# Encoder layer with expert-choice MoE on one core: the last stage summed in PSUM for all four column quarters

## The chip, the cores and the metric

The kernel runs on one core of a Trainium2 chip. The metric is the device time of one execution in microseconds (us), the median of several runs. The engines are TensorE (PE in the profile, with its weight loads as PEld), VectorE (DVE), ScalarE (ACT), GpSimd (POOL) and SyncE (SP), which issues most of the transfers. Matmuls of fp32 operands appear in the profile as two records each, those of fp32r operands as one.

## The reference, cut to what matters

One layer: three token mixers, a residual LayerNorm, then an expert-choice mixture of 16 SwiGLU experts and a second residual LayerNorm. There are 512 tokens of width 1024; each expert takes 64 tokens.

```python
def expert_choice_ffn(x, w_router, w_gate_up, w_down):
    ...
    gate, idx = lax.top_k(jnp.swapaxes(aff, 1, 2), cap)
    xs = x[bidx, idx]
    h = jnp.einsum('becd,edf->becf', xs, w_gate_up)
    hg, hu = jnp.split(h, 2, axis=-1)
    ye = jnp.einsum('becf,efd->becd', jax.nn.silu(hg) * hu, w_down)
    ye = ye * gate[..., None].astype(ye.dtype)
    return jnp.zeros_like(x).at[bidx, idx].add(ye)
...
ffn = expert_choice_ffn(x, w_router[l], w_gate_up[l], w_down[l])
x = layer_norm(DN_ALPHA * x + ffn, ln2_g[l], ln2_b[l])
```

`layer_norm` subtracts the mean over the 1024 columns, divides by the deviation (the square root of variance plus 1e-5), multiplies by a gain row g and adds a bias row b.

## The kernel before, in words

Instructions go to each engine in program order; the order of the program text is the order of every engine's queue. PSUM has eight banks of 128x512 fp32, handed out in turn under four tags: `mm` (3 banks), `S` (2), `T` (2) and `Y` (1). A new tile of a tag waits until the readers of the tile that had its bank are done.

The experts' weights come by a ring of SBUF tiles (`Ring`, L749): each `get` hands out a loaded piece, each `done` lets SP issue the next load. In order: for each expert eight pieces of gate and up weights and, for the expert before, four pieces of down weights; at the end the four down pieces of expert 14 and the four of expert 15. The pieces of expert 15 are laid out by column quarters: piece q holds all the rows of `w_down` for columns 256q to 256q+255.

Per expert e: `gate_up` (L1194) multiplies the gathered tokens (64 columns of `xs`) with gate and up weights, two column halves of 512 side by side into partitions 0-63 and 64-127 of a bank; `act_h` (L1208) makes the activation; `h_transpose` (L1217) turns it by TensorE; `down` (L1226) makes the 64 x 1024 product, split by `hi_lo` (L84) into an fp32r part and an fp32r remainder (a cast on ScalarE, a subtraction on VectorE). For every pair of experts `combine` (L1297) spreads the 128 rows to the tokens with a one-hot matrix (`slots_T`, L1252) and adds them to the accumulators `ACC[0]`, `ACC[1]` (each 128 x 2 x 1024, two blocks of 128 tokens; they start as the scaled residual). `rows_of_norm` (L1310, run in expert 12) puts the second LayerNorm's gain into `g2` and gain and bias as fp32r rows into `gb`.

The last pair (experts 14 and 15) isn't combined that way but in `last_down` (L1340), by column quarters q of 256:

- `product(q)` (L1356): expert 15's down product for quarter q. For each of eight row blocks kk it issues two matmuls of 128 columns, o = 0 and 1, into partitions 64o to 64o+63, in bank `yq` of tag S for even q, T for odd q.
- `split(q)` (L1365): the product into `yh` and `yl`, two casts and two subtractions of 64x128.
- `add(q)` (L1378), for quarters 0 and 1: eight fp32r matmuls of 256 columns into two banks, then VectorE adds them to the accumulators and takes the statistics (`bn_stats`) from SBUF; POOL multiplies by the gain (`times_g`, L1374).
- `add_in_psum(q)` (L1390), for quarters 2 and 3: the eight matmuls add to banks `xq` in which `preload` (L1334, called in expert 15, L1533 and L1538) has put the accumulators by an fp32 product with the identity. Statistics and gain are then read from PSUM by VectorE (L1397, L1400).

Then mean and variance are put together (`bn_aggr`, L1429), the reciprocal deviation y is made by square root, reciprocal and one refining step (L1430 to L1435), and -mean*y, in two fp32r parts beside ones, is written to `ch`, transposed to rows (L1442) and copied (L1444). A matmul with K = 6 of these rows and `gb` (`low_rank`, L1453) gives -mean*y*g + b for every token and column. For five of the eight output pieces (128 tokens x 512 columns, 256 KB) VectorE forms x*y plus that (`by_dve`, L1466) and SP sends them. For the three others (first column half of token blocks 0 to 2) TensorE forms diag(y) times x in fp32 (`diag`, L1458), ScalarE copies the sum (`by_act`, L1471) and sends it. `keep_warm` (L1406) issues matmuls whose results nothing reads, 22 of them after the last add and three before `low_rank`.

Of the kernel before, what the change touches and what calls it, by code (L numbers as in the profile page):

```python
# [9 lines left out]
F32 = mybir.dt.float32  # L10
# [31 lines left out]
def layer_kernel(ctx: ExitStack, tc: tile.TileContext, xt, xn, first0, wu, bgate, rpb, gains, wrt,  # L42
# [201 lines left out]
    gb = cp.tile([6, D], F32R, name="gb")  # L244
# [972 lines left out]
    def h_transpose(e, tp=None):  # L1217
        h = HT[e]
        tp = tp or PB("mm", f"ht{e}", (P, 4, P))
        for c in range(4):  # L1220
            nc.tensor.transpose(tp[:, c], h[:, c * P:(c + 1) * P], ident)  # L1221
        t = R("A6", [P, 4, P], f"hT{e}") if e == NEXP - 1 else R("tmp", [P, 4, P], f"hT{e}", bufs=2)
        HT[e] = t
        nc.vector.tensor_copy(t, tp)  # L1224
# [85 lines left out]
    def rows_of_norm(g2):  # L1310
# [4 lines left out]
        sl, cc = (small([6, 1], n, bufs=1) for n in ("gb_s", "gb_c"))  # L1315
        nc.vector.tensor_tensor(sl, ident[:6, 4:5], ident[:6, 5:6], op=ALU.add)
        nc.vector.tensor_scalar(cc, sl, -2.0, 1.0, op0=ALU.mult, op1=ALU.add)
        sel = small([32, 8, 6], "gb_sel", bufs=1)
        for i in range(2):
            nc.vector.tensor_copy(sel[:, :, i:6:2], ident[:32, 16 + 8 * i:24 + 8 * i, None].to_broadcast([32, 8, 3]))  # L1320
        for h in range(2):
            c = slice(h * 512, h * 512 + 512)
            raw = PB("mm", f"gbr{h}")
            for j in range(4):
                nc.tensor.matmul(raw[:6, j * P:(j + 1) * P], sel[:, 4 * h + j], lnr, start=True, stop=True)
            u = R("t", [P, 512], f"gbu{h}", bufs=2)
            nc.scalar.copy(gb[:, c], raw[:6])
            nc.vector.tensor_scalar(u[:6], gb[:, c].bitcast(F32), cc, None, op0=ALU.mult)
            nc.vector.scalar_tensor_tensor(gb[:, c], raw[:6], sl, u[:6], op0=ALU.mult, op1=ALU.add)
            yield  # L1330

    quarters = [slice(q * 256, q * 256 + 256) for q in range(4)]

    def preload(q, banks):  # L1334
        r = [PB(b, f"xq{q}{mp}", (P, 2, 256)) for mp, b in enumerate(banks)]
        for mp in range(2):
            nc.tensor.matmul(r[mp], ident, ACC[mp][:, :, quarters[q]], start=True, stop=False)
        return r

    def last_down(g2, xq, spare):  # L1340
# [9 lines left out]
        yy = [PB(b, f"yq{b}") for b in "ST"]  # L1350
        cbs = [spare, PB("Y", "cbl")]

        def part(q, o):
            return yy[q % 2][o * 64:o * 64 + 64, (q // 2) * P:(q // 2) * P + P]

        def product(q):  # L1356
            w = [x[:, c] for x in ring.get("dn", e, q) for c in range(4)]
            for kk in range(8):
                hf, c = divmod(kk, 4)
                for o in range(2):  # L1360
                    nc.tensor.matmul(part(q, o), hT[:, c, hf * 64:hf * 64 + 64], w[kk][:, o * P:(o + 1) * P],
                                     start=(kk == 0), stop=(kk == 7))
            ring.done("dn", e, q)

        def split(q):  # L1365
            r = slice(64, 128)
            b = cols[q].start
            cs = [slice(b + o * P, b + (o + 1) * P) for o in range(2)]
            for o in range(2):
                nc.scalar.copy(yh[r, cs[o]], part(q, o))  # L1370
            for o in range(2):
                nc.vector.tensor_tensor(yl[r, cs[o]], part(q, o), yh[r, cs[o]].bitcast(F32), op=ALU.subtract)

        def times_g(mp, q):  # L1374
            x = ACC[mp][:, :, cols[q]]
            nc.gpsimd.tensor_tensor(x, x, g2[:, None, cols[q]].to_broadcast([P, 2, 256]), op=ALU.mult)  # L1376

        def add(q):  # L1378
            for m in range(NT):
                cb = cbs[m // 2][:, m % 2 * 256:m % 2 * 256 + 256]  # L1380
                nc.tensor.matmul(cb, g[:, m], yh[:, cols[q]], start=True, stop=False)
                nc.tensor.matmul(cb, g[:, m], yl[:, cols[q]], start=False, stop=True)
            for mp in range(2):
                x = ACC[mp][:, :, cols[q]]
# [38 lines left out]
        add_in_psum(3)  # L1423
        for mp in range(2):
            times_g_psum(2, mp)
        keep_warm(22)
# [3 lines left out]
        nc.scalar.activation(sg, mv[:, :, 1], AF.Sqrt, bias=eps)  # L1430
        nc.vector.tensor_scalar(hv, mv[:, :, 1], LN_EPS, -0.5, op0=ALU.add, op1=ALU.mult)
# [4 lines left out]
        nc.vector.scalar_tensor_tensor(nm, mv[:, :, 0], -1.0, y, op0=ALU.mult, op1=ALU.mult)  # L1436
        nc.vector.tensor_copy(ch[:, :, 0:5:4], nm[:, :, None].to_broadcast([P, NT, 2]))
        nc.vector.tensor_tensor(ch[:, :, 2], nm, ch[:, :, 0].bitcast(F32), op=ALU.subtract)
        dg = R("tmp", [P, NT, P], "dgr", bufs=2)
        tp = PB("Y", "rowT", (P, NT, P))  # L1440
        for m in range(NT):
            nc.tensor.transpose(tp[:6, m], ch[:, m].bitcast(F32), ident)  # L1442
        rows = R("t", [P, 512], "rows", F32R, bufs=2)
        nc.scalar.copy(rows[:6], flat(tp)[:6])  # L1444
        keep_warm(3)
        for m in range(3):
            nc.scalar.activation(dg[:, m], ident, AF.Copy, scale=y[:, m:m + 1])
        for mp in range(2):
            times_g_psum(3, mp)
        bank = {(0, 1): "T", (1, 1): "S", (2, 1): "mm", (3, 1): "mm", (3, 0): "S", (0, 0): "T", (1, 0): "mm", (2, 0): "Y"}  # L1450
        tl = {}

        def low_rank(m, h, start=True):  # L1453
            if start:
                tl[m, h] = PB(bank[m, h], f"lr{m}{h}")
            nc.tensor.matmul(tl[m, h], rows[:6, m * P:(m + 1) * P], gb[:, h * 512:h * 512 + 512], start=start, stop=True)

        def diag(m):  # L1458
            tl[m, 0] = PB(bank[m, 0], f"lr{m}0")
            nc.tensor.matmul(tl[m, 0], dg[:, m], acc_of(m)[:, 0:512], start=True, stop=False)  # L1460

        def store(m, h):
            c = slice(h * 512, h * 512 + 512)
            (nc.sync if h else nc.scalar).dma_start(out[:, m, c], acc_of(m)[:, c])

        def by_dve(m, h):  # L1466
            x = acc_of(m)[:, h * 512:h * 512 + 512]
            nc.vector.scalar_tensor_tensor(x, x, y[:, m:m + 1], tl[m, h], op0=ALU.mult, op1=ALU.add)
            (nc.sync).dma_start(out[:, m, h * 512:h * 512 + 512], x)

        def by_act(m):  # L1471
            x = acc_of(m)[:, 0:512]
            nc.scalar.copy(x, tl[m, 0])
# [195 lines left out]
```

## Time and profile before

| | us |
|---|---|
| runs: median (lowest to highest of 3) | 982.35 (980.65 to 982.48) |
| the profiled execution, whole | 982.14 |
| its span in the profile | 980.3 |
| weights of expert 15 first used in `last_down` | 948.66 |
| last piece of output issued | 977.52 |

| engine | busy us | share of the span |
|---|---|---|
| TensorE (PE) | 957.3 | 98% |
| VectorE (DVE) | 451.6 | 46% |
| ScalarE (ACT) | 269.2 | 27% |
| GpSimd (POOL) | 75.2 | 8% |

A row of the timeline gives start, length, engine, line, operation, the tile written and the tiles read, shapes, a count of merged instructions, and in brackets the engine's idle time before it and what ended that. Lengths of matmul records hold the way through the array; how many fit into a stretch is read from the starts. The chain of waits goes back from the last instruction to what released each step. The mean granted TensorE clock over the whole span is 0.996 of full speed.

### The profile page before, as it was taken

How to read it: one execution, taken by the hardware profiler on the slowest of the kernel's cores; microseconds unless marked ns; L12 is line 12 of the kernel's file. 1: busy time of each engine (PE TensorE's matmuls, PEld its weight loads, DVE VectorE, ACT ScalarE, POOL GpSimd, SP SyncE). 2: the span in 40 equal slices, each digit the busy share in tenths (PEclk: the TensorE clock that was granted, in tenths of full speed). 3: DMA queues.
4: the chain of work that ended last, by engine and by line, in shares of the span. 5: the costliest groups of instructions: out<-in, count | busy, mean ns of one | idle time of the engine just before them, and what ended most of it. 6: DMA issues, size and time to landing. Idle time of an engine off the chain costs nothing.

```text
span 980.3 us, 13446 instructions
## 1 busy us (share of the span) xinstructions
PE 957.3 (98%) x5448; PEld 624.2 (64%) x5448; DVE 451.6 (46%) x852; ACT 269.2 (27%) x531; POOL 75.2 (8%) x82
## 2 busy tenths in 40 slices
PE   8999899999999999999999999999999999999997
PEld 8899787889888888887885334433343333432355
DVE  6347677665376566246473155331332223231336
ACT  5334345444354454233232010100010001100021
POOL 0002403000032231000021000000000000000001
PEclk9999999999999999999999999999999999999998
DMA  9322111211333322675639999999999999999992
GB/s 356 110 66 66 65 65 43 65 46 64 95 109 103 98 81 87 215 287 204 239 122 421 393 426 427 425 427 426 427 426 425 428 425 427 427 426 426 427 388 86
DMA packets 52318, 251.61 MB, mean 257 GB/s; under 512 B 14080, under 2 KB 14496, under 8 KB 28704
## 3 DMA queue, kind: packets, MB, share of 16 engines
q1 hardware_dynamic: 51680, 249.44, 64.2%
q10 hardware_dynamic: 576, 1.31, 0.3%
q8 instruction: 43, 0.70, 0.3%
q14 instruction: 19, 0.16, 0.0%
HBM read 247.84 MB, written 2.10 MB: 255 GB/s over the span
## 4 chain that ended last, share of the span: by engine, by line
PE 79%; DMA 8%; DVE 6%; ACT 2%; POOL 2%; issue 1%; SPq 0%; DVEq 0%; POOLq 0%; ACTq 0%
PE g L1203 10%; PE u L1203 9%; PE y L1236 8%; DMA gu<-in_wgu 6%; PE gate L253 4%; PE gate L254 4%; PE gate L255 4%; DMA dn<-in_wdn 2%; PE cb L1304 2%; PE ga L1168 1%; PE nqk L253 1%; PE nqk L255 1%; PE nqk L254 1%; PE gy L608 1%; PE pr L253 1%
## 5 line engine op out<-in xcount | busy, mean ns | idle before, releaser
L1203 PE MATMUL g<-gu,xs 128*64 128x512 f32 x512 | 134.7, 604 | 1.2 <-DMA gu<-in_wgu 1.1
L1203 PE MATMUL u<-gu,xs 128*64 128x512 f32 x512 | 131.6, 592 | 0.0
L1236 PE MATMUL y<-dn,hT 128*64 128x512 f32 x480 | 106.4, 593 | 2.4 <-DMA dn<-in_wdn 2.3
L85 ACT CAST y<-y 64x512 fp32r<-64x512 f32 x30 | 17.4, 579 | 241.2 <-PE y L1236 211.3
L86 DVE TENSOR_TENSOR y<-y,y 64x512 fp32r<-64x512 f32 x30 | 20.7, 689 | 136.4 <-ACT y L85 136.4
L1203 PEld LDWEIGHTS u<-gu,xs 128*64 128x64 f32 x512 | 36.8, 137 | 73.1 <-issue 71.7
L1236 PEld LDWEIGHTS y<-dn,hT 128*64 128x64 f32 x480 | 34.0, 137 | 71.5 <-issue 63.5
L86 DVE TENSOR_TENSOR lo_twin<-raw_twin,whi 128x1024 fp32r<-128x1024 f32 x43 | 53.8, 1252 | 51.9 <-ACT whi L85 51.8
L85 ACT CAST whi<-raw_twin 128x1024 fp32r<-128x1024 f32 x64 | 67.2, 1051 | 17.5 <-PE wo L1017 8.7
L1203 PEld LDWEIGHTS g<-gu,xs 128*64 128x64 f32 x512 | 31.3, 136 | 56.0 <-issue 45.3
L1307 DVE TENSOR_TENSOR acc<-acc,cb 128x512 f32<-128x512 f32 x56 | 35.5, 683 | 35.1 <-PE cb L1305 35.1
L86 DVE TENSOR_TENSOR wlo<-raw_twin,whi 128x1024 fp32r<-128x1024 f32 x21 | 27.2, 1295 | 36.8 <-ACT whi L85 36.7
L253 PE MATMUL gate<-xha,whi 128*128 128x512 f32 x96 | 39.0, 406 | 0.0
L1376 POOL TENSOR_TENSOR acc<-acc,ln2g 128x512 f32<-128x512 f32 x4 | 5.1, 1279 | 435.4 <-DVE l2s L1387 435.3
L254 PE MATMUL gate<-xla,whi 128*128 128x512 f32 x96 | 37.5, 391 | 0.0
L253 PE MATMUL gate<-xhb,whi 128*128 128x512 f32 x96 | 37.3, 389 | 0.0
L254 PE MATMUL gate<-xlb,whi 128*128 128x512 f32 x96 | 37.3, 389 | 0.0
L584 ACT ACTIVATE P_twin<-gs,nm 128x512 f32<-128x512 f32 x32 | 21.7, 683 | 52.3 <-DVE nm L583 52.3
L1224 DVE COPY hT<-ht 128x512 f32<-128x512 f32 x15 | 10.4, 690 | 53.9 <-PE ht L1221 53.9
L1213 ACT ACTIVATE tg<-g 128x512 f32<-128x512 f32 x16 | 9.6, 597 | 89.1 <-PE g L1203 89.1
L255 PE MATMUL gate<-xha,lo_twin 128*128 128x512 f32 x80 | 31.2, 390 | 0.0
L255 PE MATMUL gate<-xhb,lo_twin 128*128 128x512 f32 x80 | 31.1, 389 | 0.0
(439 smaller groups left out, 1960.9 us busy)
## 6 DMA issues: line engine op xcount, KB each, us to landing
gu<-in_wgu SPq DMA_DIRECT2D x123, 1024.0 KB
dn<-in_wdn SPq DMA_DIRECT2D x59, 1024.0 KB
raw_twin<-in_wu SPq DMA_DIRECT2D x65, 512.0 KB
gu<-in_wgu SPq DMA_DIRECT2D x10, 512.0 KB
dn<-in_wdn SPq DMA_DIRECT2D x10, 512.0 KB
raw<-in_wu SPq DMA_DIRECT2D x8, 512.0 KB
xr<-in_xt SPq DMA_DIRECT2D x4, 512.0 KB
x<-in_xn SPq DMA_DIRECT2D x2, 1024.0 KB
```

Source lines behind the costliest of these rows:

```text
L85: nc.scalar.copy(hi, src)
L86: nc.vector.tensor_tensor(lo, src, hi.bitcast(F32), op=ALU.subtract)
L253: nc.tensor.matmul(acc, w_h, rh[:, k], start=(k == 0), stop=False)
L254: nc.tensor.matmul(acc, w_h, rl[:, k], start=False, stop=False)
L255: nc.tensor.matmul(acc, w_l, rh[:, k], start=False, stop=(k == nk - 1))
L584: nc.scalar.activation(self.p[:, h], self.s[h], AF.Exp, bias=nm[:, h:h + 1], accum_out=self.sm[:, h:h + 1])
L608: nc.tensor.matmul(self.y[h * 64:h * 64 + 64, :P], ST["vg"][:, kc, kvh * 64:kvh * 64 + 64], self.pt[:, h, kc], start=(kc == 0), stop=(kc = ...
L1203: nc.tensor.matmul(GU[e][b][hf * 64:hf * 64 + 64], xs, w[b][:, hf * 512:hf * 512 + 512], start=(k == 0), stop=(k == KD - 1))
L1224: nc.vector.tensor_copy(t, tp)
L1236: nc.tensor.matmul(y[o * 64:o * 64 + 64], hT[:, c, hf * 64:hf * 64 + 64], w[j][:, o * 512:(o + 1) * 512], start=(k == 0 and j == 0), stop= ...
L1304: nc.tensor.matmul(cb, g[:, m], yh[:, c], start=True, stop=False)
L1307: nc.vector.tensor_tensor(a, a, cb, op=ALU.add)
```

## The change

All four quarters are now summed in PSUM on the residual. In expert 15 the accumulators are split by quarters into two fp32r parts (`split_acc`), in SBUF tiles whose weights are used up, and `preload` puts them into PSUM with four fp32r matmuls a quarter by an fp32r identity, made in expert 12. Quarters 0 and 1 are preloaded in expert 15, quarter 2 after product 0, quarter 3 after the third add. `product(q)` uses one matmul of 256 columns for each kk, into partitions 64(q mod 2) onward of a single bank `yq`; the cast and subtraction of a split are 64x256.

Quarters 0 to 2 are copied to SBUF by ScalarE and multiplied by the gain on POOL (`scaled`); quarter 3 as before on VectorE (`scaled_last`). The first column half is put back into PSUM by an fp32 product with the identity (`put`), and K = 12 rows, -mean*g + deviation*b there and -mean*y*g + b for the second half, are added by `low_rank`. ScalarE finishes the first half by one multiplication with y, VectorE the second. The 22 warming matmuls and the products with diag(y) are gone. The diff, cut to its core:

```diff
...
+    ACCP = {}
+
+    def split_acc(q, tag):
+        ACCP[q] = t = R(tag, [P, 2, NT, 256], f"accp{q}", F32R)
+        for mp in range(2):
+            m2 = slice(2 * mp, 2 * mp + 2)
+            hi_lo(t[:, 0, m2], t[:, 1, m2], ACC[mp][:, :, quarters[q]])
+
     def preload(q, banks):
-        r = [PB(b, f"xq{q}{mp}", (P, 2, 256)) for mp, b in enumerate(banks)]
+        t = ACCP.pop(q)
+        r = [PB(b, f"xq{q}{mp}", (P, 2, 256)) if isinstance(b, str) else b for mp, b in enumerate(banks)]
         for mp in range(2):
-            nc.tensor.matmul(r[mp], ident, ACC[mp][:, :, quarters[q]], start=True, stop=False)
+            for n in range(2):
+                nc.tensor.matmul(r[mp], ident_r, t[:, n, 2 * mp:2 * mp + 2], start=(n == 0), stop=False)
         return r
 
...
-        yy = [PB(b, f"yq{b}") for b in "ST"]
-        cbs = [spare, PB("Y", "cbl")]
-
-        def part(q, o):
-            return yy[q % 2][o * 64:o * 64 + 64, (q // 2) * P:(q // 2) * P + P]
+        r = slice(64, 128)
+        yq = PB("S", "yq")
+
+        def part(q):
+            b = 64 * (q % 2)
+            return yq[b:b + 64, (q // 2) * 256:(q // 2) * 256 + 256]
 
         def product(q):
             w = [x[:, c] for x in ring.get("dn", e, q) for c in range(4)]
             for kk in range(8):
                 hf, c = divmod(kk, 4)
-                for o in range(2):
-                    nc.tensor.matmul(part(q, o), hT[:, c, hf * 64:hf * 64 + 64], w[kk][:, o * P:(o + 1) * P],
-                                     start=(kk == 0), stop=(kk == 7))
+                nc.tensor.matmul(part(q), hT[:, c, hf * 64:hf * 64 + 64], w[kk], start=(kk == 0), stop=(kk == 7))
             ring.done("dn", e, q)
 
         def split(q):
-            r = slice(64, 128)
-            b = cols[q].start
-            cs = [slice(b + o * P, b + (o + 1) * P) for o in range(2)]
-            for o in range(2):
-                nc.scalar.copy(yh[r, cs[o]], part(q, o))
-            for o in range(2):
-                nc.vector.tensor_tensor(yl[r, cs[o]], part(q, o), yh[r, cs[o]].bitcast(F32), op=ALU.subtract)
-
...
         def add(q):
-            for m in range(NT):
-                cb = cbs[m // 2][:, m % 2 * 256:m % 2 * 256 + 256]
-                nc.tensor.matmul(cb, g[:, m], yh[:, cols[q]], start=True, stop=False)
-                nc.tensor.matmul(cb, g[:, m], yl[:, cols[q]], start=False, stop=True)
-            for mp in range(2):
-                x = ACC[mp][:, :, cols[q]]
-                nc.vector.tensor_tensor(x, x, cbs[mp].rearrange("p (a b) -> p a b", a=2), op=ALU.add)
-                for m in (2 * mp, 2 * mp + 1):
-                    nc.vector.bn_stats(st[:, m, q], acc_of(m)[:, cols[q]])
-                times_g(mp, q)
-
-        def add_in_psum(q):
             for n in range(2):
                 for m in range(NT):
                     nc.tensor.matmul(xq[q][m // 2][:, m % 2], g[:, m], (yh, yl)[n][:, cols[q]], start=False,
@@ -1396,98 +1388,96 @@
         def stats(q, m):
             nc.vector.bn_stats(st[:, m, q], xq[q][m // 2][:, m % 2])
 
-        def times_g_psum(q, mp):
-            nc.vector.tensor_tensor(ACC[mp][:, :, cols[q]], xq[q][mp], g2[:, None, cols[q]].to_broadcast([P, 2, 256]),
-                                    op=ALU.mult)
-
-        def flat(t):
-            return t[:, :, :].rearrange("p a b -> p (a b)")
-
-        def keep_warm(n):
-            for _ in range(n):
-                nc.tensor.matmul(spare[:, :P], ident, ident, start=True, stop=True)
+        def scaled(q):
+            for mp in range(2):
+                x = ACC[mp][:, :, cols[q]]
+                nc.scalar.copy(x, xq[q][mp])
+                nc.gpsimd.tensor_tensor(x, x, g2[:, None, cols[q]].to_broadcast([P, 2, 256]), op=ALU.mult)
+
+        def scaled_last(q):
+            for mp in range(2):
+                nc.vector.tensor_tensor(ACC[mp][:, :, cols[q]], xq[q][mp],
+                                        g2[:, None, cols[q]].to_broadcast([P, 2, 256]), op=ALU.mult)
+
+        tl = {}
+
+        def put(m, bank):
+            tl[m, 0] = PB(bank, f"fin{m}")
+            nc.tensor.matmul(tl[m, 0], ident, acc_of(m)[:, 0:512], start=True, stop=False)
 
         product(0)
         split(0)
+        xq[2] = preload(2, (spare.rearrange("p (a b) -> p a b", a=2), "Y"))
         product(1)
         split(1)
         add(0)
+        for m in range(NT):
+            stats(0, m)
+        scaled(0)
         product(2)
         split(2)
         add(1)
+        for m in range(NT):
+            stats(1, m)
+        scaled(1)
         product(3)
-        add_in_psum(2)
+        add(2)
+        xq[3] = preload(3, ("T", "S"))
+        split(3)
         for m in range(NT):
             stats(2, m)
-        split(3)
-        add_in_psum(3)
-        for mp in range(2):
-            times_g_psum(2, mp)
-        keep_warm(22)
+        add(3)
+        scaled(2)
+        put(0, "mm")
+        put(1, "mm")
+        put(2, "S")
+        put(3, "T")
         for m in range(NT):
             stats(3, m)
             nc.vector.bn_aggr(mv[:, m], st[:, m])
-        nc.scalar.activation(sg, mv[:, :, 1], AF.Sqrt, bias=eps)
-        nc.vector.tensor_scalar(hv, mv[:, :, 1], LN_EPS, -0.5, op0=ALU.add, op1=ALU.mult)
+        mean, var = mv[:, :, 0], mv[:, :, 1]
+        nc.scalar.activation(sg, var, AF.Sqrt, bias=eps)
+        nc.vector.tensor_scalar(hv, var, LN_EPS, -0.5, op0=ALU.add, op1=ALU.mult)
+        nc.vector.tensor_scalar(ch[:, :, 6:11:4], mean[:, :, None].to_broadcast([P, NT, 2]), -1.0, None, op0=ALU.mult)
+        nc.vector.scalar_tensor_tensor(ch[:, :, 8], mean, -1.0, ch[:, :, 6].bitcast(F32), op0=ALU.mult, op1=ALU.subtract)
         nc.vector.reciprocal(y, sg)
         nc.vector.tensor_tensor(a, y, y, op=ALU.mult)
         nc.vector.tensor_tensor(a, a, hv, op=ALU.mult)
         nc.vector.scalar_tensor_tensor(y, a, 1.5, y, op0=ALU.add, op1=ALU.mult)
-        nc.vector.scalar_tensor_tensor(nm, mv[:, :, 0], -1.0, y, op0=ALU.mult, op1=ALU.mult)
+        nc.vector.scalar_tensor_tensor(sg, hv, -2.0, y, op0=ALU.mult, op1=ALU.mult)
+        nc.gpsimd.tensor_copy(ch[:, :, 7:12:4], sg[:, :, None].to_broadcast([P, NT, 2]))
+        nc.gpsimd.tensor_tensor(ch[:, :, 9], sg, ch[:, :, 7].bitcast(F32), op=ALU.subtract)
+        nc.vector.scalar_tensor_tensor(nm, mean, -1.0, y, op0=ALU.mult, op1=ALU.mult)
         nc.vector.tensor_copy(ch[:, :, 0:5:4], nm[:, :, None].to_broadcast([P, NT, 2]))
         nc.vector.tensor_tensor(ch[:, :, 2], nm, ch[:, :, 0].bitcast(F32), op=ALU.subtract)
-        dg = R("tmp", [P, NT, P], "dgr", bufs=2)
         tp = PB("Y", "rowT", (P, NT, P))
         for m in range(NT):
-            nc.tensor.transpose(tp[:6, m], ch[:, m].bitcast(F32), ident)
+            nc.tensor.transpose(tp[:12, m], ch[:, m].bitcast(F32), ident)
         rows = R("t", [P, 512], "rows", F32R, bufs=2)
-        nc.scalar.copy(rows[:6], flat(tp)[:6])
-        keep_warm(3)
-        for m in range(3):
-            nc.scalar.activation(dg[:, m], ident, AF.Copy, scale=y[:, m:m + 1])
-        for mp in range(2):
-            times_g_psum(3, mp)
-        bank = {(0, 1): "T", (1, 1): "S", (2, 1): "mm", (3, 1): "mm", (3, 0): "S", (0, 0): "T", (1, 0): "mm", (2, 0): "Y"}
-        tl = {}
-
-        def low_rank(m, h, start=True):
-            if start:
-                tl[m, h] = PB(bank[m, h], f"lr{m}{h}")
-            nc.tensor.matmul(tl[m, h], rows[:6, m * P:(m + 1) * P], gb[:, h * 512:h * 512 + 512], start=start, stop=True)
-
-        def diag(m):
-            tl[m, 0] = PB(bank[m, 0], f"lr{m}0")
-            nc.tensor.matmul(tl[m, 0], dg[:, m], acc_of(m)[:, 0:512], start=True, stop=False)
-
-        def store(m, h):
-            c = slice(h * 512, h * 512 + 512)
-            (nc.sync if h else nc.scalar).dma_start(out[:, m, c], acc_of(m)[:, c])
-
-        def by_dve(m, h):
+        nc.scalar.copy(rows[:12], tp[:12].rearrange("p a b -> p (a b)"))
+        tl[0, 1] = PB("mm", "lr0")
+        for _ in range(3):
+            nc.tensor.matmul(tl[0, 1][:, :P], ident, ident, start=True, stop=True)
+        scaled_last(3)
+
+        def low_rank(m, h):
+            nc.tensor.matmul(tl[m, h], rows[:12, m * P:(m + 1) * P], gb[:, h * 512:h * 512 + 512], start=bool(h), stop=True)
+
+        def finish(m, h):
             x = acc_of(m)[:, h * 512:h * 512 + 512]
-            nc.vector.scalar_tensor_tensor(x, x, y[:, m:m + 1], tl[m, h], op0=ALU.mult, op1=ALU.add)
-            (nc.sync).dma_start(out[:, m, h * 512:h * 512 + 512], x)
-
-        def by_act(m):
-            x = acc_of(m)[:, 0:512]
-            nc.scalar.copy(x, tl[m, 0])
-            nc.scalar.dma_start(out[:, m, 0:512], x)
-
-        low_rank(3, 0)
-        low_rank(0, 1)
-        low_rank(1, 1)
-        diag(0)
-        low_rank(0, 0, False)
-        low_rank(2, 1)
-        low_rank(3, 1)
-        diag(1)
-        low_rank(1, 0, False)
-        diag(2)
-        low_rank(2, 0, False)
-        for k in ((3, 0), (0, 1), (1, 1), (2, 1), (3, 1)):
-            by_dve(*k)
-        for m in range(3):
-            by_act(m)
+            if h:
+                nc.vector.scalar_tensor_tensor(x, x, y[:, m:m + 1], tl[m, h], op0=ALU.mult, op1=ALU.add)
+            else:
+                nc.scalar.activation(x, tl[m, h], AF.Copy, scale=y[:, m:m + 1])
+            (nc.scalar if (m, h) == (3, 0) else nc.sync).dma_start(out[:, m, h * 512:h * 512 + 512], x)
+
+        for m in range(NT):
+            low_rank(m, 0)
+            if m:
+                tl[m, 1] = PB("TSY"[m - 1], f"lr{m}")
+            low_rank(m, 1)
+            finish(m, 0)
+            finish(m, 1)
 
...
+            split_acc(0, "VS")
+            split_acc(1, "E0")
             gate_up(e, (0, 1))
-            x2 = preload(2, "ST")
+            x0 = preload(0, "ST")
             gate_up(e, (2, 3))
             h_transpose(e - 1)
             slots_T(e // 2)
+            split_acc(2, "A2")
+            split_acc(3, "A3")
             gate_up(e, (4, 5))
-            x3 = preload(3, ("mm", "mm"))
+            x1q = preload(1, ("mm", "mm"))
             gate_up(e, (6, 7))
             spare = PB("mm", "spare")
...
-    ch = small([P, NT, 6], "ch", F32R, bufs=1)
+    ch = small([P, NT, 12], "ch", F32R, bufs=1)
...
-    last_down(g2, {2: x2, 3: x3}, spare)
+    last_down(g2, {0: x0, 1: x1q}, spare)
```

Expert 12 also gets `ident_r` (one cast of the identity), a `gb` of 12 rows instead of 6, with zeros for the other column half, and selectors of that width in `rows_of_norm`.

More of the change, by code (lines that the diff above doesn't have):

```diff
@@ L243, in layer_kernel @@
     lnr = cp.tile([32, P], F32, name="lnr")
-    gb = cp.tile([6, D], F32R, name="gb")
+    gb = cp.tile([12, D], F32R, name="gb")
     nc.sync.dma_start(lnr, lnp.rearrange("a (j n) -> (a j) n", n=P))
@@ L1221, in h_transpose @@
             nc.tensor.transpose(tp[:, c], h[:, c * P:(c + 1) * P], ident)
[L1222 removed]
+        t = R("A0", [P, 4, P], f"hT{e}") if e == NEXP - 1 else R("tmp", [P, 4, P], f"hT{e}", bufs=2)
         HT[e] = t
@@ L1508, in layer_kernel @@
                 g2 = R("A5", [P, D], "ln2g")
+                ident_r = R("A6", [P, P], "ident_r", F32R)
+                nc.scalar.copy(ident_r, ident)
                 side = rows_of_norm(g2)
```

27 lines of the change are left out of this document (15 added, 12 removed).

## Prediction

> **What bounds the kernel now.** I read the busy time by stretches first, then the chain of waits in order of time, then the timeline of the end. Times are us from the start of the profiled execution, whose span is 980.3. In the stretches the columns are length, busy time of PE, PEld, DVE, ACT and POOL with counts, granted TensorE clock, DMA share, GB/s.
>
> ```profile
> 940.00:948.60 8.60, 8.37 (x40) 2.62 (x36) 2.16 (x6) 2.17 (x4) 0.00 (x0) 1.00 1.01 421
> ...
> 970.50:971.00 0.50, 0.50 (x2) 0.29 (x2) 0.50 (x2) 0.00 (x0) 0.00 (x0) 1.00 0.05 20
> ...
> 970.90:975.00 4.10, 4.10 (x7) 1.33 (x7) 1.92 (x3) 1.17 (x2) 0.00 (x0) 0.62 1.00 384
> ...
> 978.30:979.10 0.80, 0.00 (x0) 0.00 (x0) 0.00 (x0) 0.00 (x0) 0.00 (x0) 0.50 0.84 328
> ```
>
> Until 948.6 the weights stream without a break, and the stage can't start before they land. In the chain of waits:
>
> ```profile
> 928.95 19.57 DMA dn<-in_wdn
> ...
> 948.66 1.97 PE yqS L1361 x32
> 950.62 1.76 PE yqT L1361 x32
> ...
> 959.95 1.33 DVE l2s L1397 x4
> ...
> 961.94 0.74 PE xq L1393 x4
> ...
> 974.10 2.01 PE lr L1460 x2
> ```
>
> The first piece is the weights' landing, then come two products, then VectorE (adds and statistics, with the last subtraction queued behind them), and at the end TensorE at a low clock: a mean of 0.62 from 970.9 to 975 is full clock up to about 971.9 and 0.50 from there. The timeline shows the handovers:
>
> ```profile
> 925.30 1.98 PE L1337 MATMUL xq<-acc,ident 128*128 128x512 f32 x4
> ...
> 927.21 1.08 PE L1203 MATMUL g<-gu,xs 128*64 128x512 f32 x4
> ...
> 928.12 1.03 PE L1203 MATMUL u<-gu,xs 128*64 128x512 f32 x4
> ...
> 950.42 1.94 PE L1361 MATMUL yqT<-dn,hT 128*64 128x128 f32 x32
> ...
> 952.30 0.39 PE L1381 MATMUL spare<-y,GT 128*128 128x256 f32 x1
> ...
> 953.24 0.28 PE L1382 MATMUL cbl<-y,GT 128*128 128x256 f32 x1
> ...
> 956.79 1.97 PE L1361 MATMUL yqT<-dn,hT 128*64 128x128 f32 x32 [0.17 <-DMA dn<-in_wdn]
> ...
> 961.29 0.59 DVE L1372 TENSOR_TENSOR y<-yqT,y 64x128 fp32r<-64x128 f32 x2
> ...
> 963.12 0.42 DVE L1397 BATCH_NORM_STATS2 l2s<-xq 128x6 f32<-128x256 f32 x1
> ...
> 965.32 0.26 DVE L1429 BATCH_NORM_AGGREGATE l2mv<-l2s 128x2 f32<-128x24 f32 x1
> ...
> 965.62 0.30 ACT L1430 ACTIVATE l2v<-l2mv,eps 128x4 f32<-128x4 f32 x1 [6.29 <-DVE l2mv L1429]
> 965.95 0.18 DVE L1432 RECIPROCAL l2y<-l2v 128x4 f32<-128x4 f32 x1 [0.16 <-ACT l2v L1430]
> ...
> 967.16 0.17 DVE L1438 TENSOR_TENSOR ch<-l2m,ch 128x4 fp32r<-128x4 f32 x1
> ...
> 968.10 0.57 ACT L1444 CAST rows<-rowT 6x512 fp32r<-6x512 f32 x1 [2.19 <-PE rowT L1442]
> ...
> 968.73 0.96 PE L1456 MATMUL lr<-gb,rows 6*128 6x512 f32 x3
> ...
> 969.35 3.51 DVE L1468 SCALAR_TENSOR_TENSOR acc<-acc,l2y,lr 128x512 f32<-128x512 f32 x5 [0.83 <-PE lr L1456]
> ...
> 970.12 3.10 SPq L1469 DMA_DIRECT2D out<-acc  x5
> ...
> 971.26 0.58 ACT L1473 COPY acc<-lr 128x512 f32<-128x512 f32 x1 [1.69 <-issue]
> ...
> 977.52 0.34 ACTq L1474 DMA_DIRECT2D out<-acc  x1
> ```
>
> The last product ends at 956.79 + 1.76 = 958.55, but its subtraction starts only at 961.29. That VectorE queue is what the change takes away. The last three outputs leave late because the fp32 product with the diagonal and the K = 6 product run at clock 0.50.
>
> **Up to 948.66: nothing.** Expert 15 gets eight casts on ScalarE and eight subtractions on VectorE (the accumulators in two parts), and its preloads become eight fp32r matmuls. The rows below price them.
>
> ```profile
> 914.24 0.40 PE L1304 MATMUL cb<-y,GT 128*128 128x512 f32 x1
> ...
> 914.47 0.40 PE L1305 MATMUL cb<-y,GT 128*128 128x512 f32 x1
> ...
> 931.49 0.69 DVE L1224 COPY hT<-ht 128x512 f32<-128x512 f32 x1 [7.47 <-PE ht L1221]
> ...
> 931.77 0.58 ACT L1259 CAST GT<-gT 128x512 fp32r<-128x512 f32 x1 [11.34 <-PE gT L1256]
> ```
>
> Eight times 0.58 and eight times 0.69 fit into the idle 11.34 and 7.47 in front of these two rows and into what follows them. An fp32r matmul of 512 columns costs 0.23 (914.24 to 914.47), so a quarter preloads in 0.95 instead of 1.91 (925.30 to 927.21). TensorE gets ahead and then waits for the same transfers. Were that cover gone, the first preload would wait for its second subtraction, 0.7 at most, less than the two preloads save. The small additions at expert 12 (one cast, wider selectors) lie under the same stream. No transfer is added, moved or delayed on SP's queue, and hT's new place and the four tiles for the parts hold weights that are used up by then.
>
> **The products: the term that decides.** Today each kk issues two matmuls of 128 columns to the two 64-column halves of the array. A product takes 1.76 (948.66 to 950.42): 32 records, two for each fp32 matmul, or 16 steps of 0.11, each 128 columns in both halves at once. That they overlap follows from two rows: four full-width records of 512 columns take 1.91 (0.43 to 0.48 each), four half-width ones 0.91 to the next group (927.21 to 928.12), so two half-width records go in the time of one. The new product puts all 256 columns into one half (`part(q)` is one partition half) with 8 matmuls, 16 records of 256 columns, nothing beside them: 16 × 0.2165 = 3.46. Bounds: 1.73, if all still overlapped, and 3.8, by the preload's slower 0.48 per 512 columns. I take 3.46.
>
> The Trainium skill, "TensorE: Matmul & The Clock Gate", section "Part 3: Packing small matmuls — row/col tiling", says that small-M matmuls run concurrently only when their outputs lie in different column groups, and measures 2.38 for three of them rather than 3. That speaks against this change, but for less: as an estimate two halves would gain 2 × 2.38 / 3 = 1.59, a product would be 2.75, and the total 985.8 - 4 × 0.71 = 983.0. The trace's ratio here is about 2, and the measurement decides.
>
> TensorE's order is product 0, preload 2, product 1, add 0, product 2, add 1, product 3, add 2, preload 3, add 3, in one queue. An add is 8 matmuls of 256 columns at 0.119 (952.30 to 953.24 for seven steps): 0.95. Changing between half and full width costs 0.12 to 0.14 (950.42 + 1.76 to 952.30), seven times, 0.95. Sum: 4 × 3.46 + 2 × 0.95 + 4 × 0.95 + 0.95 = 20.5, so the last add ends near **969.2**. Today its last half starts at 961.94 and ends at 962.7.
>
> What could hold it: all products now lie in one bank, so a product waits until the one before has been split. A split is one cast and one subtraction of 64x256. These groups of today bound them:
>
> ```profile
> L1370 ACT CAST y<-yqS 64x128 fp32r<-64x128 f32 x4 | 1.0, 259 | 2.9 <-PE yqS L1361 2.9
> ...
> L85 ACT CAST y<-y 64x512 fp32r<-64x512 f32 x2 | 1.2, 580 | 6.8 <-PE y L1236 6.1 <-DVE y L86 0.8
> ...
> L1372 DVE TENSOR_TENSOR y<-yqS,y 64x128 fp32r<-64x128 f32 x4 | 1.2, 290 | 0.2
> ...
> L86 DVE TENSOR_TENSOR y<-y,y 64x512 fp32r<-64x512 f32 x2 | 1.4, 689 | 4.2 <-ACT y L85 4.2
> ```
>
> Between them I take 0.37 and 0.42. With 0.3 for hops and the drain that is 1.1, and the preload or add in between, 0.95 with two changes of width, 1.2, covers it. At the upper end, 0.58 + 0.69 + 0.3, each of three products is held by some 0.35, 1.1 in all; at the lower end nothing. VectorE no longer adds, and TensorE is its only source: statistics of quarters 0 to 2 are done before 969. The copies to SBUF and POOL's multiplications by the gain end before the first half is put back. Those four fp32 matmuls, at the preload's 0.95 each, run from 969.2 to 973.0 under the last statistics, in place of the 22 warming ones.
>
> **From the last add to the end.** Statistics start near 969.2, six matmuls into the last add, and take 965.58 - 963.12 = 2.46: 971.66. Then 1.75 as today (to 967.33), and 0.47 more: two extra instructions beside the square root overrun it by 0.27, one more stands in the chain at 0.20 (965.95 to 967.16 holds six steps). POOL's two for the deviation run beside VectorE's last three. The nearest POOL rows are
>
> ```profile
> L997 POOL TENSOR_SCALAR lnr<-r_y 128x2 f32<-128x2 f32 x1 | 0.2, 232 | 106.4 <-DVE r_y L969 106.4
> ...
> L247 POOL TENSOR_SCALAR gT<-lnT 128x8 f32<-128x8 f32 x1 | 0.8, 818 | 0.3 <-DMA lnT<-in_lnt 0.3
> ```
>
> At 0.3 each they end 0.1 after VectorE, at 0.8 they cost 1.1. I take the former: 973.95. Transposes and rows as today (967.33 to 968.73): lr at 975.35. Its result reaches an engine 0.62 later (968.73 to 969.35). ScalarE's first piece takes 0.58, and SP issues it 0.07 later, 976.6. Should the clock have fallen by then, as it has today, a matmul takes up to 0.3 longer, which I leave to the range.
>
> From there transfers decide. Four pieces each from ScalarE (0.58) and VectorE (0.70) come every 0.35, and a piece of 256 KB takes 0.66: 2.10 MB at 400 GB/s, 5.24. The start lag is 0.86: issued at 970.12, and DMA busy for 0.05 of the half microsecond before 971. For the last piece 977.52 + 0.86 + 0.67 (0.84 of 0.8) gives its last byte at 979.05, and 1.25 later the span ends. End: 976.6 + 0.86 + 5.24 + 1.25 = **984.0**, 3.7 over today. Around the span this execution had 1.84 (982.14 in all), so **985.8**, 3.5 above the median of 982.35, from which 982.14 differs by 0.2. Bounds of the transfer rate, 384 and 421 GB/s, are +0.2 and -0.3.
>
> **Rivals.** B, faster: the products stay at 1.73, because the array takes one half's stream at the paired rate. Then TensorE's sum is 13.6, the last add ends at 962.3, and everything behind comes 6.9 sooner: **978.9**. It decides as soon as a product is under 2.5. For it: VectorE's queue is really gone. Against: the two rows on the widths. C, no change: the output isn't bound by transfers, and the last piece sets the end. VectorE's fourth ends near 979.0, issue at 979.1, then 0.86 + 0.66 + 1.25 = 981.9, **983.7**. Against: 384 GB/s held from 970.9 to 975 with both queues in use. D: the one bank holds each product at the upper price, **986.9**. For it: the cover is barely as long as the split. E: the half-used array lets the clock fall to 0.50 during the products. The clock fell at the end under K = 6 matmuls, but never in this trace under half-width pairs. Three products and their adds doubled: about **998**. F: a half alone overlaps partly, product midway at 2.6: **982.4**. The skill's 2.75 in the section named is near it.
>
> **How the numbers follow.** Forecast 64%, B 8%, C 13%, D 10%, E 2%, F 3%. The forecast's own range is 984.4 to 987.5 (transfer rate, clock, POOL). Taken to C and D it is 982.8 to 988.0, leaving out B, E, F and some tail. About 0.2%, 2 us, is what a measurement tells from no change: 980.4 to 984.3. Slower: 61 of the 64 points, D and E, 73%. Same: C, F and the forecast's 3, 19%. Faster: B, 8%.
>
> **What would show it.** A product of 16 records in 3.4 to 3.5 with no overlap; the last add ending at 968.5 to 970; no adds on VectorE, which waits for TensorE before each statistic; TensorE free of waits for weights after product 0; some 5 us of unbroken output at 400 GB/s. A product near 1.8, or idle TensorE between products, would break the forecast.

## The result, and the profile after

| | before | after |
|---|---|---|
| runs side by side: median (lowest to highest of 4) | 981.6 (980.65 to 982.48) | 986.75 (986.13 to 988.45) |
| the profiled execution, whole | 982.14 | 987.14 |
| its span | 980.3 | 985.3 |
| first product of `last_down` | 948.66 | 950.29 |
| from there to the end of the span (called the stage below) | 31.64 | 35.01 |

The changed kernel takes 1.0056 of the time before, with an interval from 1.0039 to 1.0073: slower by 3.8 to 7.2 us. The forecast was 985.8, from 982.8 to 988.0. Of the stage it had said 984.0 - 948.66 = 35.3; it took 35.0.

First the chain of waits of the changed kernel in order of time (start, length, what), from the weights' landing to the three warming matmuls ahead of `low_rank` (six records, 976.03):

```profile
930.26 19.90 DMA dn<-in_wdn
...
950.29 3.64 PE yq L1376 x16
953.93 0.66 PE spare L1352 x2
...
955.05 3.60 PE yq L1376 x16
958.65 1.14 PE xq L1385 x8
959.79 3.60 PE yq L1376 x16
963.39 1.14 PE xq L1385 x8
964.53 3.60 PE yq L1376 x16
...
970.21 0.72 PE xq L1385 x6
...
970.96 0.44 DVE l2s L1389
...
973.17 0.27 DVE l2mv L1437
...
975.43 0.60 PE rowT L1455 x4
976.03 0.67 PE lr L1460 x6
```

From 950.29 to 970.94 every piece is TensorE's, and each begins where the one before ends: four products, the preloads and the adds. Before, VectorE's adds and statistics stood in the middle of this chain; now VectorE enters only behind the last add, with the last statistics. The timeline shows that nothing else holds the products, and how the end goes:

```profile
958.69 0.37 ACT L85 CAST y<-yq 64x256 fp32r<-64x256 f32 x1 [4.35 <-PE yq L1376]
959.09 0.43 DVE L86 TENSOR_TENSOR y<-yq,y 64x256 fp32r<-64x256 f32 x1 [4.31 <-ACT y L85]
...
975.12 0.17 DVE L1452 TENSOR_TENSOR ch<-l2m,ch 128x4 fp32r<-128x4 f32 x1
975.13 0.22 POOL L1449 TENSOR_TENSOR ch<-l2v,ch 128x4 fp32r<-128x4 f32 x1
...
977.98 4.04 SPq L1472 DMA_DIRECT2D out<-acc  x7
```

The cast and the subtraction of product 1 end at 959.52, while the add of quarter 0, which TensorE does next, runs until 959.79, so the bank is free before product 2 wants it. POOL's last write ends at 975.35, 0.06 after VectorE's. The busy time by stretches (length, busy time of PE, PEld, DVE, ACT, POOL with counts, granted clock, DMA share, GB/s) shows the stage and two places ahead of it:

```profile
11.50:15.00 3.50, 3.50 (x17) 3.50 (x18) 2.54 (x3) 1.05 (x1) 0.00 (x0) 0.51 1.02 417
522.00:526.00 4.00, 3.98 (x48) 3.52 (x49) 2.30 (x8) 0.00 (x1) 0.00 (x0) 0.69 0.98 378
950.30:971.00 20.70, 20.70 (x105) 13.85 (x105) 7.38 (x19) 5.46 (x12) 5.38 (x5) 1.00 0.24 100
971.00:978.80 7.80, 6.97 (x28) 3.75 (x26) 6.35 (x23) 2.59 (x6) 2.52 (x4) 1.00 0.00 0
978.90:984.00 5.10, 0.00 (x0) 0.00 (x0) 1.34 (x3) 0.79 (x2) 0.00 (x0) 0.70 1.05 405
```

TensorE is busy for all of the 20.7 us of products and sums, at full clock; the output then runs without a break at 405 GB/s. The first two rows lie in code that the change doesn't touch: at these places this execution ran at half clock (from 522 to 526 for part of it), and the execution of before did not (1.00 in both). That bears on the base, which the experiments take up.

### The profile page after: what moved, and what is told of

It is laid out like the page before. It is cut to its first block, busy times and chain, and to the rows that moved or that the text cites. A ratio compares the mean times of both kernels' runs of the same rounds, so it can differ in the third digit from the quotient of the medians.

```text
span 985.3 us, 13277 instructions
## 1 busy us (share of the span) xinstructions
PE 959.3 (97%) x5350; PEld 624.4 (63%) x5350; DVE 451.8 (46%) x855; ACT 276.4 (28%) x540; POOL 77.6 (8%) x86
## 4 chain that ended last, share of the span: by engine, by line
PE 76%; DMA 12%; DVE 6%; ACT 2%; POOL 2%; issue 1%; SPq 0%; DVEq 0%; POOLq 0%; ACTq 0%
PE g L1203 9%; PE u L1203 8%; PE y L1236 8%; DMA gu<-in_wgu 8%; PE gate L253 4%; DMA dn<-in_wdn 4%; PE gate L254 4%; PE gate L255 4%; PE nqk L253 1%; PE nqk L255 1%; PE nqk L254 1%; PE yq L1376 1%; PE gy L608 1%; PE pr L253 1%; PE ga L1168 1%
## 5 line engine op out<-in xcount | busy, mean ns | idle before, releaser
L86 DVE TENSOR_TENSOR y<-y,y 64x512 fp32r<-64x512 f32 x30 | 20.7, 689 | 136.9 <-ACT y L85 136.9
L1395 POOL TENSOR_TENSOR acc<-acc,ln2g 128x512 f32<-128x512 f32 x6 | 7.5, 1268 | 443.7 <-ACT acc L1394 443.7
```

The costliest lines, as they stand in the source:

```text
L86: nc.vector.tensor_tensor(lo, src, hi.bitcast(F32), op=ALU.subtract)
```

## Experiments

Each kernel's median stands beside that of the kernel before on the same chip: 981.42 (31 runs, 979.24 to 985.32) for the first four, 981.01 (17 runs, 979.47 to 984.09) for the last two. Single executions of one kernel scatter by several us, so parts are also compared by the stage as defined above, from one profiled execution each.

### The changed kernel once more

> The changed kernel once more, with the kernel before beside it. The profiled execution of it that was seen first began the last stage at 950.29, 1.63 us later than before, and the granted clock had halved twice for some 3.5 us in code that the change doesn't touch (11.6 to 15 and 522 to 526 us). Theory: that shift is chance, so an execution without these two dips starts the last stage within 0.5 us of 948.66 and ends near a span of 983.7. Rival: the longer program itself delays the weights, and the last stage starts 1.2 us or more late in an execution without dips too.

Measured: 986.91 (983.86 to 988.74, 10 runs), ratio 1.0046 (1.0031 to 1.0061). The profiled execution took 983.86, its span 982.1. From its chain of waits:

```profile
947.01 3.64 PE yq L1376 x16
```

The stage is 982.1 - 947.01 = 35.1, as in the first execution of the changed kernel. Its start is 3.3 earlier than there, and this execution was at full clock at both places where the first had run at half (1.00 from 11.5 to 15 and from 522 to 526). So the rival falls: the longer program doesn't delay the start in this execution. The theory's number missed as well: 948.66 within 0.5 was expected, and the start came 1.65 earlier than that. Where the start lies is decided ahead of the changed stage.

### Both halves of the array again, everything else as changed

```diff
-        def part(q):
-            b = 64 * (q % 2)
-            return yq[b:b + 64, (q // 2) * 256:(q // 2) * 256 + 256]
+        def part(q, o):
+            return yq[o * 64:o * 64 + 64, q * P:(q + 1) * P]
...
-                nc.tensor.matmul(part(q), hT[:, c, hf * 64:hf * 64 + 64], w[kk], start=(kk == 0), stop=(kk == 7))
+                for o in range(2):
+                    nc.tensor.matmul(part(q, o), hT[:, c, hf * 64:hf * 64 + 64], w[kk][:, o * P:(o + 1) * P],
+                                     start=(kk == 0), stop=(kk == 7))
```

A split is two casts and two subtractions again.

> The changed kernel with its product issued as before: two matmuls of 128 columns into the two column halves of the array, all else as changed (the split is again two casts and two subtractions). Theory (the unpaired product is the whole loss): a product takes 1.76 instead of 3.60, four of them 7.4 less; the wait for the last weights and the holds by the single product bank give back some 1 us, so the last add ends some 14.4 us after the stage's start instead of 20.9, and the kernel is 6 us faster than the changed one and about 3 us (0.3%) faster than before. Rival (the sum in PSUM with its preloads on TensorE, or the new end, costs as much): the gain over the changed kernel stays under 3 us and the kernel is not faster than before.

Measured: 979.71 (978.09 to 982.35, 12 runs), ratio 0.998 (0.9967 to 0.9994). The span is 979.0. From the chain of waits:

```profile
950.04 1.98 PE yq L1376 x32
...
953.26 1.99 PE yq L1376 x32
...
957.31 0.58 ACT acc L1400
...
957.97 0.58 ACT acc L1400
...
963.85 0.72 PE xq L1391 x6
```

And two rows of its timeline, which follow each other:

```profile
959.80 1.97 PE L1376 MATMUL yq<-dn,hT 128*64 128x128 f32 x32 [0.20 <-DVE y L1386]
961.69 0.51 PE L1391 MATMUL spare<-y,GT 128*128 128x256 f32 x2
```

From its start to the start of what follows, a product now takes 1.89 (959.80 to 961.69) instead of 3.60, the last add ends at 964.57, 14.5 after the start instead of 20.65, and the stage is 979.0 - 950.04 = 28.96: 6.1 less than with one half. By the ratios it is (1.0046 - 0.998) x 981.4 = 6.5. This one edit makes the changed kernel faster than the one before; the product's shape is what the change lost by. The row of product 3 also shows what the single bank costs once products are short: it waits for the split of product 2, whose casts stood behind two copies of quarter 0 on ScalarE's queue (957.31 and 957.97).

### The new end alone, on the kernel before

```diff
-        keep_warm(22)
+        put(0, "S")
+        put(1, "T")
+        put(2, "S")
+        put(3, "T")
```

From `mean` on, with the 12 rows, the code is the changed kernel's; products, adds and quarters are those of before.

> The kernel before with the change's end alone: first column half put back into PSUM, K = 12 rows, ScalarE finishing by a multiplication; products, adds and preloads as before (the four put-backs use other banks, since the ones of the change hold the third and fourth quarter here). Theory: the end, from the last statistic on, is 2.8 us shorter, since the three pieces that waited for the diagonal products at half clock now leave at the pace of the transfers: 0.28% faster than before. Rival: the end is bound by the output transfers either way and the longer chain of small operations eats the rest: within 0.1% of before.

Measured: 979.4 (978.05 to 981.1, 12 runs), ratio 0.9982 (0.9969 to 0.9995). The span is 976.3. From the chain of waits:

```profile
947.41 1.97 PE yqS L1366 x32
...
966.35 0.60 PE rowT L1461 x4
...
967.61 0.49 PE fin L1469
```

And from the stretches:

```profile
967.60:969.80 2.20, 2.14 (x9) 1.39 (x8) 1.42 (x3) 1.61 (x3) 0.00 (x0) 1.00 0.02 7
969.80:975.10 5.30, 0.00 (x0) 0.00 (x0) 1.30 (x2) 0.81 (x2) 0.00 (x0) 0.52 1.02 393
```

The stage is 28.89, against 31.64 in the profiled execution of before. TensorE is through with the last products in 2.2 us at full clock; only then does the clock fall, with no TensorE work left. The output leaves at 393 GB/s. So the end is a gain: by the ratio the kernel is 1.8 us faster than before (0.5 to 3.0).

### The unpaired product alone, on the kernel before

```diff
-        def part(q, o):
-            return yy[q % 2][o * 64:o * 64 + 64, (q // 2) * P:(q // 2) * P + P]
+        def part(q):
+            b = 64 * (q % 2)
+            return yy[q % 2][b:b + 64, (q // 2) * 256:(q // 2) * 256 + 256]
```

With it go the one matmul of 256 columns and the split by `hi_lo`; both banks stay.

> The kernel before with the change's product alone: 8 matmuls of 256 columns into one column half, the split one cast and one subtraction of 64x256, two product banks as before. Theory: products of 3.60 instead of 1.76 make TensorE the bound, the third add waits behind the fourth product and VectorE's statistics of the third quarter stand ahead of the last split: 6 to 7 us (0.65%) slower than before. Rival: VectorE's queue of adds bounds this stage whatever TensorE does, and it hides most of the longer products: under 3 us slower.

Measured: 986.08 (984.34 to 988.75, 10 runs), ratio 1.0044 (1.0029 to 1.0059): 4.3 us slower by the ratio, as much as the whole change. The span is 982.5. From the timeline of TensorE:

```profile
947.69 2.99 PE L1361 MATMUL yqS<-dn,hT 128*64 128x256 f32 x13 [0.33 <-DMA dn<-in_wdn]
950.31 0.43 PE L1361 MATMUL yqT<-dn,hT 128*64 128x256 f32 x1
950.52 0.38 PE L1361 MATMUL yqS<-dn,hT 128*64 128x256 f32 x1
950.58 0.38 PE L1361 MATMUL yqT<-dn,hT 128*64 128x256 f32 x1
...
951.01 2.97 PE L1361 MATMUL yqT<-dn,hT 128*64 128x256 f32 x13
953.91 0.38 PE L1375 MATMUL spare<-y,GT 128*128 128x256 f32 x1
```

Products 0 and 1 stand back to back here, in different halves of the array and different banks, and the last three records of the one alternate with the first three of the other: together they take 6.2 (947.69 to 953.91), where 3.46 twice and one change of width would be 7.1. The loss is smaller than the 6 to 7 that were expected, and this overlap is one reason, worth 0.8; how much VectorE's queue still hides of the rest was not worked out. The stage is 982.5 - 947.69 = 34.8. In this execution the clock held to the end of TensorE's work, so it is compared with an execution of before in which it held too; the next three look for one.

### The kernel before, three more executions

Nothing is edited.

> The kernel before, unchanged, for another profiled execution (three are taken). The stage lengths from its first product to the end of the span are 31.6 us before and 35.0 changed, 3.4 apart, but the medians differ by 5.5. Theory: in the execution of before that was seen first the clock halved at 971.9, under the diagonal products; where it falls later, these take 2.2 us less (they did in the unpaired-only kernel, where the clock held), so the stage of before lasts from 29.4 to 31.6 and is shorter the later the clock falls. Rival: the stage of before lasts 31.6 within 0.3 whatever the clock, and the rest of the median's difference lies ahead of the stage.

> As for the first of the three: 29.4 to 31.6 us from the first product to the end, by when the clock falls; the rival says 31.6 within 0.3.

> As for the first of the three: 29.4 to 31.6 us from the first product to the end, by when the clock falls; the rival says 31.6 within 0.3.

Measured: 983.42, 983.87 and 982.77, with spans of 981.6, 982.0 and 981.0 and stages from 950.60, 950.44 and 951.54: 31.0, 31.56 and 29.46. The stretches of the first execution, around its warming matmuls and behind them:

```profile
950.60:964.90 14.30, 12.52 (x161) 11.46 (x162) 11.63 (x28) 3.04 (x10) 5.12 (x4) 0.97 0.33 140
964.90:971.10 6.20, 6.20 (x47) 6.15 (x46) 5.02 (x19) 0.30 (x1) 0.00 (x0) 0.79 0.01 3
971.10:978.60 7.50, 7.00 (x25) 3.10 (x22) 3.47 (x5) 3.05 (x7) 0.00 (x0) 1.00 0.57 220
```

Those of the second, with one row from far ahead of the stage:

```profile
100.00:103.50 3.50, 3.50 (x19) 3.50 (x18) 2.91 (x10) 1.26 (x6) 0.00 (x0) 0.52 0.00 0
...
964.40:969.30 4.90, 4.90 (x46) 4.86 (x45) 4.36 (x18) 0.30 (x1) 0.00 (x0) 1.00 0.01 3
969.30:978.50 9.20, 9.20 (x25) 3.57 (x24) 4.48 (x7) 2.63 (x6) 0.00 (x0) 0.74 0.52 200
```

And of the third:

```profile
965.50:970.40 4.90, 4.90 (x46) 4.85 (x45) 4.36 (x18) 0.30 (x1) 0.00 (x0) 1.00 0.02 3
970.40:977.50 7.10, 7.07 (x25) 3.16 (x24) 4.48 (x7) 2.64 (x6) 0.00 (x0) 1.00 0.53 205
```

The same end of before, 44 warming records and 25 of the tail, takes 4.9 + 7.1 with the clock held, 4.9 + 9.2 where it falls in the tail, and 6.2 + 7.5 where it falls under the warming matmuls and recovers. The rival falls with the third execution. So the stage of before has no one length: in these four executions it lies between 29.5 and 31.6, and the execution that the prediction used is at the long end. Against the held clock, the unpaired product costs 34.8 - 29.46 = 5.35, and the new end saves 29.46 - 28.89 = 0.57; against the fallen one the new end saves 31.64 - 28.89 = 2.75.

These executions also bear on why the stage starts at different times. Of the ten profiled executions of all kernels here, the four that start it earliest (947.0 to 948.7) are at full clock from 11.5 to 15, from 100 to 103.5 and from 522 to 526; the six that start it at 950.0 or later each have at least one of these stretches at 0.51 to 0.69. The shift is there long before the last stage: SP issues the transfer of L433 (`v_shift`, far ahead of the experts) at 252.3 to 253.1 in the four and at 254.3 to 256.4 in the six. The times of the other runs go the same way. Of the 48 runs of before that stand beside the experiments, the 17 with a mean granted clock of 1.0 took 979.24 to 980.85, and the seven with 0.994 or less 982.39 to 985.32.

### Both halves and two banks

On the kernel with both halves: products go to banks S and T in turn, and the preload of quarter 2 moves behind product 1.

```diff
-            return yq[o * 64:o * 64 + 64, q * P:(q + 1) * P]
+            return yy[q % 2][o * 64:o * 64 + 64, (q // 2) * P:(q // 2) * P + P]
...
         split(0)
-        xq[2] = preload(2, (spare.rearrange("p (a b) -> p a b", a=2), "Y"))
         product(1)
         split(1)
+        xq[2] = preload(2, (spare.rearrange("p (a b) -> p a b", a=2), "Y"))
```

> The changed kernel with paired products in two banks in turn, as before, and the third quarter's preload after product 1 instead of between the first two. With one bank a product waited for the split of the one before it, and the third split for ScalarE's copies; last add ended 14.5 us after the stage's start. Theory (the holds by the one bank cost about 1 us): the last add ends 13.5 after the start, the stage lasts 28 us, and the kernel is about 0.3% faster than before and 0.1% faster than with one bank. Rival: TensorE's own sum, or the landing of the last weights, bounds the stage, and two banks change it by less than 0.3 us.

Measured: 979.76 (977.36 to 981.6, 12 runs), ratio 0.9985 (0.9973 to 0.9996). The span is 978.1. From the chain of waits:

```profile
950.12 1.97 PE yqS L1376 x32
952.09 1.75 PE yqT L1376 x32
...
955.90 1.92 PE yqS L1376 x32
```

And from the timeline:

```profile
962.76 1.11 PE L1391 MATMUL xq<-y,GT 128*128 128x256 f32 x8
963.71 2.74 PE L1412 MATMUL fin<-acc,ident 128*128 128x512 f32 x6
```

The last add ends 13.6 after the start and the stage is 28.0, 1.0 less than with one bank, as expected. The times don't show it: against before the kernel is 0.15% faster (0.04% to 0.27%), not 0.3%, and no faster than with one bank (ratios 0.9985 and 0.998, medians 979.76 and 979.71, each beside its own runs of before). With single executions spread over 4 us, a microsecond isn't told apart. How much of it is the second bank and how much the new order, which saves two changes of width between products 0 and 1, was not tried separately.

## Why the prediction was right

| step | predicted | measured |
|---|---|---|
| a product with one change of width | 3.46 + 0.135 | 3.60 |
| start to the end of the last add | 20.5 | 20.65 |
| last statistics, mean and variance | 2.46 | 2.49 (970.96 to 973.45) |
| from there to the last write of `ch` | 2.29 | 1.90 (to 975.35) |
| from there to the first `low_rank` | 1.40 | 1.34 (to 976.69) |
| from there to the first piece's issue | 1.25 | 1.29 (to 977.98) |
| from there to the end of the span | 7.4 | 7.3 |
| stage | 35.3 | 35.0 |

**Up to the stage: nothing.** Right: in the changed kernel the stage still starts when the last weights land (the DMA row at the head of the chain of waits). The split of the accumulators delays nothing that shows in the starts: those of the kernel before lie from 948.66 to 951.54, 950.29 among them, and 947.01 is earlier than all of them.

**The products.** The deciding term was right, and the runs isolate it: with only this edit undone the stage is 6.1 shorter, and with only this edit made on the kernel before it is 5.35 longer (clock held in both). The rule that the prediction set beside its row, "Part 3: Packing small matmuls — row/col tiling" in "TensorE: Matmul & The Clock Gate" of the Trainium skill, would have given a pair a gain of some 1.6 as an estimate; here it is 1.9 with the change of width in both (3.60 to 1.89), and 1.98 without it (3.46, which is 3.60 less one change, to the 1.75 of the second product in the last experiment). The row of before was the better guide. The size of the term owes something to luck: the prediction's 0.2165 for a record of 256 columns stands beside no row. Its rows give 0.22 (two steps of 0.11) and 0.24 (half of the preload's 0.48), and what came is (3.60 - 0.135) / 16 = 0.217.

**The single bank.** Right that its hold is covered in the changed kernel, though by 0.27 only (959.52 against 959.79). In the kernel with both halves, with splits of four instructions and short products, it isn't covered: there products 1 and 3 both follow a split in the chain of waits. Rival D, which put its cost on the changed kernel, fell.

**The end.** Right in kind; the largest error is the 0.4 between the statistics and the last write of `ch`. The prediction added 0.47 there for three instructions on VectorE. The two beside the square root cost nothing: the reciprocal starts 0.38 behind the last mean and variance (973.83), as before (0.37), and not 0.27 later. The third cost 0.08, not 0.20. POOL's two were priced rightly, with their end 0.06 behind VectorE's. The end is a gain that the products outweigh. Moving all four sums to PSUM gives nothing in the form that the change has: with the new end and paired products in both, the stage is 28.96 with the sums in PSUM and one bank, 28.89 with VectorE's adds. With two banks it is 28.0. By stages the whole is 31.64 - 2.75 (new end) + 0.07 (sums in PSUM) + 6.05 (unpaired products) = 35.0.

**The rivals.** B (a product of 1.73) and F (2.6) fell with the 3.60, C with the unbroken 5.1 us of output at 405 GB/s, E with the clock of 1.00 from 950.3 to 978.8 (its sum comes to 999, not 998: three times 3.46 + 0.95 is 13.2).

**The size against the median.** This is the one piece that was off. The prediction put the changed kernel 3.5 above the median of before; side by side it is 5.2 above (3.8 to 7.2 by the interval), and 4.5 by the ratio of the larger sample (3.0 to 6.0). The step at fault is "so **985.8**, 3.5 above the median": it took a difference against one execution of before for one against the median. That execution has a stage of 31.64; the four seen average (31.64 + 31.0 + 31.56 + 29.46) / 4 = 30.9, so 0.7 of the loss was hidden in the base. The larger sample says the same: against 981.42, the median of 31 runs, 985.8 is 4.4 above. The profiled execution of the changed kernel then came out at 987.14, because its stage began 1.63 later and took 0.3 less. What is left of the difference lies inside the intervals and wasn't settled; one fall of the clock ahead of the stage moves an execution by about 2 us (the transfer of L433 above), and how often each kernel meets one isn't known.

## What to carry to other kernels

A product with 64 output rows fills half of the partitions of a PSUM bank. Two such matmuls issued in turn to the two halves took about half as long here as one after the other in one half (1.75 against 3.46), so a rewrite that saves instructions by joining them can cost more than the vector work that it removes. When single executions scatter by more than the effect, cut the span at a common event and compare the stage on its own, and look at more than one execution of the base too. A short end leaves less work for a falling clock to lengthen: from the transposes on, TensorE needed 3.4 us in the new end (966.35 to 969.75), and 7.1 or 9.2 in the old one, by whether the clock held.

## What the runs showed of the hardware that was not expected

The granted clock fell to half for 3.41 us in the middle of the program and then recovered, at places that differ between executions of one kernel. Two stretches of the second of the three further executions of before:

```profile
96.56:99.97 3.41, 1.60 (x12) 1.24 (x12) 2.83 (x8) 2.78 (x8) 0.00 (x0) 1.00 0.00 0
99.97:103.38 3.41, 3.41 (x18) 3.41 (x18) 2.82 (x9) 1.29 (x6) 0.00 (x0) 0.50 0.00 0
```

And the same two places in the execution of before that the prediction used:

```profile
96.59:100.00 3.41, 1.60 (x11) 1.01 (x11) 2.82 (x8) 2.54 (x8) 0.00 (x0) 1.00 0.00 0
100.00:103.41 3.41, 3.41 (x31) 3.41 (x31) 2.85 (x7) 1.53 (x6) 0.00 (x0) 1.00 0.00 0
```

TensorE is busy throughout the slow stretch, but not in the one ahead of it, where it waits 1.81 us for VectorE. The nine such falls in the ten executions all follow a stretch of 3.41 us in which TensorE was busy for 1.60 to 2.46 only; the one under the back-to-back warming matmuls follows the wait for the last split. Such a stretch is not enough, as the second pair of rows shows. "Part 1: The HAM clock gate (the "warmup" mystery)" in "TensorE: Matmul & The Clock Gate" of the Trainium skill has a free-running window of 3413 ns, after which an idle array is throttled. The length agrees; but here the array was idle for only part of the window ahead, and no run here shows what decides whether the clock falls.

Two products in different halves and banks also overlap where the one ends and the other begins, by three records (the alternating rows of the unpaired product alone): 0.8 us saved without any pairing in the code.
